# Conditioning products of a diffusion step: two stationary columns in one column group, or 32 padded columns in four

## The chip, the core and the metric

The kernel runs on one core of one Trainium2 chip. The metric is the device time of one execution in microseconds (us). The kernel before takes 1270.43 us, the median of 3 runs (1269.55 to 1271.19).

Engine names are those of the profile: PE is the matrix engine, PEld its weight loads, DVE the vector engine, ACT the scalar engine, POOL the GpSimd engine, SP the engine from whose queue nearly all DMAs here are issued. SPq is time in SP's queue. "Stationary" is the operand that a weight load puts into the array, "moving" the one that streams through it. A PSUM bank holds 512 fp32 numbers in each of 128 partitions.

## The reference

One step of a two-layer backbone: layer 0 has two attention mixers A and B, layer 1 a Fourier mixer. There are 256 context tokens and 1024 latent tokens of width 1024. Each layer starts from a normalised input that is scaled and shifted by vectors made from a conditioning vector, and ends with a gate made from it. There are two conditioning vectors, `c` for latent tokens and `c_ctx` for context tokens.

```python
def ada_mod(cvec, w, b):                       # w: (1024, 3072), one per layer
    m = jax.nn.silu(cvec) @ w + b
    return jnp.split(m, 3, axis=-1)            # shift, scale, gate

def modulate(h, shift, scale):
    return h * (1 + scale) + shift

for l in range(DEPTH):                         # DEPTH = 2
    shc, scc, gtc = ada_mod(c_ctx, ada_w[l], ada_b[l])
    shl, scl, gtl = ada_mod(c, ada_w[l], ada_b[l])
    hc = modulate(rms_norm(xc, norm_g[l]), shc, scc)
    hl = modulate(rms_norm(xl, norm_g[l]), shl[:, None], scl[:, None])
    # layer 0: projections of hc, hl; attention A (global) and B (window); gated output projection
    # layer 1: Fourier mixing of the projected input; gated output projection
    xc = xc + gtc * yc
    xl = xl + gtl[:, None] * yl
y_prompt, y_sample = rms_norm(xc, final_g), rms_norm(xl, final_g)
```

The change touches `silu(cvec) @ w` alone: a product of 2 vectors of 1024 with a 1024 x 3072 matrix, for each layer.

## The kernel before, in words

Tokens are cut into 10 tiles of 128 and three groups: tiles 0 to 3, 4 to 7 (latent) and 8 to 9 (context). Big products take their operands as a high and a low part (`mm3`, L246, three products for one); the conditioning products take plain fp32 operands.

All conditioning weights are cut into blocks of 128 columns. A block is one DMA from `ada_w` of 128 x 8 x 128 numbers, 512 KB (`ada_tile`, L461, pieces of 512 bytes), and one group of eight matmuls (`ada_mm`, L466), one for each 128 rows of the matrix: `cs[:, b, :]`, 128 x 2, is stationary, the block's 128 columns are moving, and the result stands in two partitions of a PSUM bank.

**Layer 0's shift and scale** are wanted first. A loop over `k` = 0 to 7 loads the two blocks of 128 columns (`ada_load`), multiplies them (`ada_chunk`, tile name `ada`, one bank `g`), copies the 2 x 256 result to SBUF on ACT (L480), turns it with two small transposes on PE (L483, `modt`) and writes column `k` of `modb` and `moda` on DVE (L485, L486). Then `mod_chunk` makes the modulated, split columns `k` of token group 0, and products of those columns with the first key weights and query weights are added into four banks, `kv0s`, `kv2s`, `q0s`, `q2s` (`gemm_chunk`, L492; three of these banks have the tag `s`, one the tag `a`), a few `k` behind.

**The rest of what is multiplied early** (gate of layer 0; shift and scale of layer 1; `AT_P`) is 24 blocks. `ada_fill` puts them among the following work by the table `AT_N`: that work (`S1`) normalises and modulates groups 1 and 2 (transposes `xt`, L397), loads cached keys, and makes the remaining keys, values and first queries. Each block has a bank `t` (tile name `ad`), an ACT copy (L822) and a small transpose (L799, `mt`) for a shift or a scale, or a DVE addition (L818) and a DMA to the DRAM tensor `gtd` for a gate. Layer 1's gate is made elsewhere, on DVE (class `Rows`).

**Buffers.** Weight blocks take buffers from the zones `p`, `pt` and `q` (4, 3 and 2 of them); tiles 8 and 9 of the input and some of the query work take theirs from the same zones. A load waits in SP's queue until the buffer's last reader is done, and all loads behind it wait too. Banks: `s` has 3, `t` has 3, `a` and `g` one each.

**Order.** Instructions are recorded in the order of the code, and a scheduler sets the order of each engine's queue from its own estimate of times. What stands in the queues is fixed when the program is built; on the chip each queue runs in order.

Then the attention follows (lines 860 to 1010), with remaining projections filled between its pieces, then the output projection and layer 1. None of its code is touched.

## Time and profile before

| | us |
|---|---|
| median of 3 runs | 1270.43 |
| the profiled execution's own time | 1269.79 |
| its span, first to last instruction | 1268.0 |
| PE busy, of the span | 1218.0 |
| DVE busy | 874.0 |
| ACT busy | 586.4 |
| POOL busy | 314.0 |

The 1.8 us between the profiled execution's own time and its span lie outside the instructions. The page divides the span into 40 slices of 31.7 us. PE is busy seven tenths of the first slice and at least eight tenths of almost every other; the DMA engines are at 0.9 or more in the first two slices and at 0.6 or less in most others. The chain of waits goes back from the last instruction to what released it, so its shares say what set the end.

A fp32 matmul of the program stands in the trace as two matmul records, each with its weight load, while a product of split operands stands as one. So a group of eight conditioning matmuls is 16 records. PE's records overlap (a matmul of 272 ns starts 109 ns after the one before), so what one costs is read from start to start and not from its length.

### The profile page before, as it was taken

To read this page: it belongs to the slowest core of one execution; us is meant where nothing else is said; L and a number is where in the kernel's file an instruction comes from. 1 tells how busy PE (TensorE), PEld (TensorE's weight loads), DVE (VectorE), ACT (ScalarE), POOL (GpSimd) and SP (SyncE) were. 2 spreads that over 40 slices of the span, in tenths; PEclk is the share of its full clock that TensorE was granted. 3 is DMA by queue.
4 is the path that set the end of the run, shared out by engine and by line. 5 is a ranking of instruction groups with operands and counts; after the bars stand their busy time and mean duration, and the time that the engine had idled before them with its cause. 6 is when DMAs were issued, how large, how long until landed. Compare 5 with 4: busy or idle time off the path is not lost.

```text
span 1268.0 us, 22014 instructions
## 1 busy us (share of the span) xinstructions
PE 1218.0 (96%) x8063; PEld 1073.5 (85%) x8063; DVE 874.0 (69%) x2036; ACT 586.4 (46%) x1179; POOL 314.0 (25%) x269
## 2 busy tenths in 40 slices
PE   7989999999999999999999988979999998999997
PEld 6767889999999999998999986868777888988886
DVE  3455388887767677666888868675775988558553
ACT  3332235655556455555665667432264324333121
POOL 2234155341322122010100012310412206335001
PEclk9999999999999999999999999989999999999999
DMA  9956522132342325234424379597312544355321
GB/s 298 310 146 170 164 75 63 50 114 82 107 134 75 106 65 167 57 105 117 117 67 150 89 200 250 157 255 214 124 45 75 168 148 142 101 163 172 132 84 67
DMA packets 175311, 168.83 MB, mean 133 GB/s; under 512 B 19753, under 2 KB 140373, under 8 KB 175202
## 3 DMA queue, kind: packets, MB, share of 16 engines
q1 hardware_dynamic: 175202, 167.41, 44.9%
q8 instruction: 64, 1.05, 0.3%
q14 instruction: 45, 0.37, 0.1%
HBM read 123.19 MB, written 44.18 MB: 132 GB/s over the span
## 4 chain that ended last, share of the span: by engine, by line
PE 83%; DMA 7%; DVE 4%; ACT 2%; issue 1%; POOL 1%; SPq 1%; POOLq 0%; DVEq 0%; ACTq 0%
PE ga L246 9%; PE of L246 9%; PE av L987 8%; PE pt L981 7%; PE q L246 7%; PE oz L246 6%; PE sL L864 4%; PE u L246 4%; PE kv L246 4%; PE ad L466 4%; PE g1E L246 4%; PE g1O L246 3%; PE sC L864 3%; PE ada L466 2%; PE g1c L246 2%; PE wa L516 2%
## 5 line engine op out<-in xcount | busy, mean ns | idle before, releaser
L984 DVE TENSOR_TENSOR pt<-pt,pt 128x512 fp32r<-128x512 f32 (+1 forms) x264 | 171.1, 658 | 42.8 <-ACT pt L258 42.4
L258 ACT ACTIVATE pt<-pt 128x512 fp32r<-128x512 f32 (+1 forms) x264 | 146.3, 576 | 81.5 <-PE pt L981 52.0
L987 PE MATMUL av<-pt,u 128*128 128x256 f32 x1008 | 168.7, 290 | 2.3 <-DVE e L999 1.5
L981 PE MATMUL pt<-identr,p 128*128 128x128 f32 x1008 | 154.8, 272 | 2.4 <-ACT e L962 1.3
L987 PEld LDWEIGHTS av<-pt,u 128*128 128x128 f32 x1008 | 139.6, 189 | 7.8 <-DVE e L999 3.0
L246 PE MATMUL q<-w,u 128*128 128x256 f32 x864 | 130.1, 287 | 0.3 <-ACT u L420 0.2
L981 PEld LDWEIGHTS pt<-identr,p 128*128 128x128 f32 x1008 | 118.4, 140 | 8.3 <-ACT e L962 1.5
L905 ACT ACTIVATE p<-p,nm 128x1280 f32<-128x1280 f32 (+1 forms) x80 | 95.4, 1192 | 62.6 <-DVE p L898 61.3
L246 PE MATMUL ga<-u,w 128*128 128x512 f32 (+1 forms) x576 | 124.2, 359 | 0.0
L246 PEld LDWEIGHTS q<-w,u 128*128 128x128 f32 x864 | 114.1, 189 | 4.4 <-DVE u L422 0.5
L246 PEld LDWEIGHTS ga<-u,w 128*128 128x128 f32 x576 | 93.6, 188 | 13.5
L264 POOL TENSOR_TENSOR w<-h,w 128x512 fp32r<-128x512 f32 x42 | 55.5, 1338 | 133.3 <-DVE w L260 96.7
L864 PE MATMUL sL<-u,q 128*128 128x512 f32 x256 | 81.0, 410 | 3.9 <-DMA q<-qd 2.3
L905 ACT ACTIVATE p<-p,NM 128x640 f32<-128x640 f32 (+2 forms) x80 | 59.1, 740 | 25.2 <-DVE p L898 25.0
L264 POOL TENSOR_TENSOR u<-h,u 128x512 fp32r<-128x512 f32 x19 | 25.8, 1363 | 171.4 <-ACT u L258 160.3
L246 PE MATMUL oz<-u,u 128*128 128x512 f32 x240 | 63.0, 397 | 3.4 <-DVE h L1180 1.6
L864 PE MATMUL sC<-u,q 128*128 128x256 f32 x320 | 63.2, 298 | 0.2 <-DMA q<-qd 0.2
L639 POOL TENSOR_TENSOR h<-h,rope 128x512 f32<-128x512 f32 (+1 forms) x18 | 21.7, 1206 | 148.7 <-ACT h L722 99.5
L246 PE MATMUL kv<-w,u 128*128 128x256 f32 x384 | 57.9, 289 | 0.0
L246 PEld LDWEIGHTS oz<-u,u 128*128 128x128 f32 x240 | 44.5, 188 | 14.6 <-issue 2.0
L898 DVE TENSOR_SCALAR_CACHE_REDUCE p<-sL 128x512 f32<-128x512 f32 x64 | 43.8, 684 | 18.4 <-PE sL L864 9.3
L898 DVE TENSOR_SCALAR_CACHE_REDUCE p<-sL,nm 128x512 f32<-128x512 f32 x64 | 47.6, 744 | 7.8 <-PE sL L864 6.5
(774 smaller groups left out, 2723.6 us busy)
## 6 DMA issues: line engine op xcount, KB each, us to landing
q<-qd SPq DMA_DIRECT2D x80, 256.0 KB
p<-i_ada_w SPq DMA_DIRECT2D x21, 512.0 KB
h<-i_w_in SPq DMA_DIRECT2D x40, 256.0 KB
h<-i_w_out SPq DMA_DIRECT2D x32, 256.0 KB
pt<-i_ada_w SPq DMA_DIRECT2D x14, 512.0 KB
qd<-q SPq DMA_DIRECT2D x22, 256.0 KB
w<-i_wuT SPq DMA_DIRECT2D x8, 512.0 KB
u<-i_x SPq DMA_DIRECT2D x8, 512.0 KB
```

The lines of the kernel that those rows point to most:

```text
L246: pe.matmul(out, a, b, start=i == 0, stop=i == n - 1)
L258: act.activation(out, in_, AF.Copy)
L264: pick("lo" + lc, lc).tensor_sub(dst_l, src, dst_h)
L466: pe.matmul(out, cs[:, b, :], raw[:, b, :], start=b == 0, stop=b == 7)
L516: pe.matmul(acc[:, i * 256 : i * 256 + 256], wu[j][:, c0 : c0 + P], f[:, j, :], start=j == 0, stop=j == 1)
L639: pick("rope", XE["rope"]).tensor_mul(t1.rearrange("p t h (b c) -> p t (h b) c", b=2), y.rearrange("p t h (b c) -> p t (h b) c", b=2), cb)
L864: pe.matmul(ps, q_at(q, s, hc), keys, start=s == 0, stop=s == 1)
L898: dve.tensor_scalar(p[i][:, end[i] : end[i] + n], ps, sign, last[i], op0=ALU.mult, op1=ALU.min, accum_out=c)
L905: act.activation(p[i][:, 0 : end[i]], p[i][:, 0 : end[i]], AF.Exp, bias=last[i], scale=-1.0, accum_out=SU[:, t, hd + i, 0:1],)
L981: pe.transpose(tp[:, jj * 256 + i * P : jj * 256 + i * P + P], p[i][:, off : off + P], ident)
L984: dve.tensor_sub(pt[:, 1, 0:n], tp[:, 0:n], pt[:, 0, 0:n])
L987: pe.matmul(acc, vv, pt[:, s, jj * 256 : jj * 256 + 256], start=c + jj + s == 0, stop=c + jj == nt - 1 and s == 1,)
```

## The change

The two vectors are padded to 32 columns with zeros (`csw`, one memset on POOL and one copy on DVE at the start). The result of a matmul then fills 32 partitions, and four matmuls that use the same 128 rows of the matrix but four different blocks of 128 columns write the four quarters of one bank's partitions: in the array they stand in four column groups of 32. In the built program the matmuls before have the same kind of placement, 128 rows by 32 columns, always at column 0; now it is at columns 0, 32, 64 and 96.

For layer 0's shift and scale the loop takes two `k` at once: four loads of 128 x 4 x 256 (pieces of 1 KB), 32 matmuls in the order row block, then column group, one ACT copy of 128 x 128, one 128 x 128 transpose and three DVE operations for both `k`. For the rest there are 24 loads of 128 x 2 x 512 (pieces of 2 KB) and 8 matmuls for each; four such steps fill one bank, now of tag `s`, which is then copied, turned and written like above, or, for the gate, added to the bias in four quarters. Number of matmuls (320) and of weight loads by DMA (40 of 512 KB) stay.

```diff
+AT_B = "s"
...
     dve.tensor_scalar(cs, cs, 0.5, None, op0=ALU.mult)
+    csw = take("e", (P, 8, 32))
+    pool.memset(csw.a, 0.0)
+    dve.tensor_copy(csw[:, :, 0:2], cs)
...
-    def ada_tile(l, part, k, tags):
-        raw = take(tags, (P, 8, P))
-        c0 = part * D + k * P
-        sp.dma_start(raw.a, I["ada_w"][l, :, c0 : c0 + P].rearrange("(b p) c -> p b c", p=P))
-        return raw
-
-    def ada_mm(out, raw):
+    def ada_mm(ps, j, b, raw, start, stop):
+        pe.matmul(ps[32 * j : 32 * j + 32, 0:P], csw[:, b, :], raw, start=start, stop=stop)
+
+    def ada_mods(l, name, ps, fill):
+        row = take("e", (P, P))
+        act.activation(row.a, ps[:, 0:P], AF.Copy)
+        tp = t_bank(name)
+        pe.transpose(tp[:, 0:P], row.a, ident)
+        drop(row)
+        fill(tp[:, 0:P].rearrange("p (j v) -> p j v", j=4)[:, :, 0:2])
+
+    def mod_shift(l, k, n, tv):
+        bb = bT[:, l, k : k + n].unsqueeze(2).to_broadcast([P, n, 2])
+        dve.tensor_add(modb[:, l, k : k + n, :], tv, bb)
+
+    def mod_scale(l, k, n, tv):
+        bb = bT1[:, l, k : k + n].unsqueeze(2).to_broadcast([P, n, 2])
+        gb = gT[:, l, k : k + n].unsqueeze(2).to_broadcast([P, n, 2])
+        dve.tensor_add(moda[:, l, k : k + n, :], tv, bb)
+        dve.tensor_mul(moda[:, l, k : k + n, :], moda[:, l, k : k + n, :], gb)
+
+    def ada_load(kk):
+        out = []
+        for hb in range(2):
+            for part in range(2):
+                raw = take(("p", "pt", "q"), (P, 4, 256))
+                c0 = part * D + kk * 256
+                sp.dma_start(
+                    raw.a, I["ada_w"][0, hb * 512 : hb * 512 + 512, c0 : c0 + 256].rearrange("(b p) c -> p b c", p=P)
+                )
+                out.append(raw)
+        return out
+
+    def ada_chunk(kk, raws):
+        ps = bank("g", f"ada{kk}")
         for b in range(8):
-            pe.matmul(out, cs[:, b, :], raw[:, b, :], start=b == 0, stop=b == 7)
-        drop(raw)
...
+            for j in range(4):
+                part, i = divmod(j, 2)
+                raw = raws[b // 4 * 2 + part]
+                ada_mm(ps, j, b, raw[:, b % 4, i * P : i * P + P], b == 0, b == 7)
+        drop(*raws)
+
+        def fill(tv):
+            mod_shift(0, 2 * kk, 2, tv[:, 0:2])
+            mod_scale(0, 2 * kk, 2, tv[:, 2:4])
+
+        ada_mods(0, f"modt{kk}", ps, fill)
...
-    todo_ada = deque((l, part, k) for l, part in AT_P for k in range(8))
...
+    todo_ada = deque((l, part, h, s) for l, part in AT_P for h in range(2) for s in range(4))
+    open_ada = []
+
+    def ada_step(l, part, h, s):
+        raw = take(AT_Z, (P, 2, 512))
+        c0 = part * D + h * 512
+        sp.dma_start(raw.a, I["ada_w"][l, s * 256 : s * 256 + 256, c0 : c0 + 512].rearrange("(b p) c -> p b c", p=P))
+        if s == 0:
+            open_ada.append(bank(AT_B, f"ad{l}{part}{h}"))
+        ps = open_ada[0]
+        for i in range(2):
+            for j in range(4):
+                ada_mm(ps, j, 2 * s + i, raw[:, i, j * P : j * P + P], s + i == 0, s + i == 4)
+        drop(raw)
+        if s < 3:
+            return
+        open_ada.pop()
+        if part < 2:
+            ada_mods(l, f"mt{l}{part}{h}", ps, lambda tv: (mod_shift, mod_scale)[part](l, 4 * h, 4, tv))
+            return
+        row, bias = take("e", (P, P)), take("e", (P, P))
+        for j in range(4):
+            c1 = 2 * D + h * 512 + j * P
+            sp.dma_start(bias[32 * j : 32 * j + 2, :], I["ada_b"][l, c1 : c1 + P].partition_broadcast(2))
+        for j in range(4):
+            rows = slice(32 * j, 32 * j + 2)
+            dve.tensor_add(row[rows, :], ps[rows, 0:P], bias[rows, :])
+            sp.dma_start(gtd[l, :, h * 512 + j * P : h * 512 + j * P + P], row[rows, :])
+        drop(row, bias)
```

The lines left out are the old loop bodies and the calls (`if k % 2 == 0:` ahead of the loads and of `ada_chunk`).

The scheduler orders the queues anew as far as the middle of the attention on A; from there PE's order is the same but for a few rows. Three places are shown. A row is the line, the operation, the written and the read tile with their buffer numbers, the size of the output, and how many equal instructions follow each other.

**PE, in the loop of layer 0's shift and scale.** `ada` are the conditioning products, `modt` the turn of their result, `kv0s`, `kv2s`, `q0s`, `q2s` the products of token group 0. Before, two groups of eight and the work around them:

```order
L492 MATMUL q0s<-w_333,u_434 128x256
L483 MATMUL modt_494<-identr,e_492 128x2 x2
L466 MATMUL ada_554<-p_550,cs 2x128 x8
L466 MATMUL ada_554<-pt_552,cs 2x128 x8
L492 MATMUL q0s<-w_334,u_434 128x256
L492 MATMUL q0s<-w_333,u_435 128x256
```

Now, the end of one set of 32 and the start of the next:

```order
L464 MATMUL ada_401<-q_399,e_115 32x128 x2
L464 MATMUL ada_401<-pt_397,e_115 32x128 x2
L464 MATMUL ada_401<-q_399,e_115 32x128 x2
L470 MATMUL modt_436<-identr,e_434 128x128
L464 MATMUL ada_537<-p_529,e_115 32x128 x2
L516 MATMUL kv0s<-w_301,u_441 128x256
L516 MATMUL kv0s<-w_302,u_441 128x256
```

Each row of two is two column groups that read the same load. 33 separate runs of conditioning products stood on PE's queue, and 25 stand there now.

**PE, around the last products of token group 0.** `xt` are the transposes of token group 1, each tile of four waited for by ACT and DVE, which make the modulated columns from it. Before, the transposes stand behind the last of the `kv0s` to `q2s` products and a gate block (`ad`):

```order
L492 MATMUL q2s<-w_333,u_578 128x256
L492 MATMUL q2s<-w_334,u_578 128x256
L492 MATMUL q2s<-w_333,u_579 128x256
L466 MATMUL ad_833<-q_829,cs 2x128 x7
L397 MATMUL xt_846<-identr,u_467 128x128
L397 MATMUL xt_846<-identr,u_468 128x128
L397 MATMUL xt_846<-identr,u_469 128x128
L397 MATMUL xt_846<-identr,u_470 128x128
L397 MATMUL xt_855<-identr,u_467 128x128
```

Now five of the eight sets of `xt` stand ahead of the last 48 of these products, and the other three among them or right behind:

```order
L401 MATMUL xt_843<-identr,u_470 128x128
L401 MATMUL xt_843<-identr,u_471 128x128
L401 MATMUL xt_843<-identr,u_472 128x128
L401 MATMUL xt_843<-identr,u_473 128x128
L516 MATMUL kv0s<-w_301,u_577 128x256
L516 MATMUL kv0s<-w_302,u_577 128x256
L516 MATMUL kv2s<-w_301,u_577 128x256
L516 MATMUL kv2s<-w_302,u_577 128x256
```

No gate block stands before the end of these products any more; three did.

**PE and ACT, at the first block of the gate.** Before, on PE (`ckt` is the turn of cached keys, `xt_981` belongs to token group 2):

```order
L397 MATMUL xt_915<-identr,u_470 128x128
L617 MATMUL ckt_927<-identr,h_924 128x128 x2
L466 MATMUL ad_938<-p_934,cs 2x128 x8
L466 MATMUL ad_953<-pt_949,cs 2x128 x8
L466 MATMUL ad_968<-q_964,cs 2x128 x8
L397 MATMUL xt_981<-identr,pt_761 128x128
```

Now (`q_1325` are the queries of token group 2):

```order
L250 MATMUL q_1325<-w_323,u_936 128x256
L464 MATMUL ad_772<-p_770,e_115 32x128 x8
L464 MATMUL ad_772<-pt_781,e_115 32x128 x8
L464 MATMUL ad_772<-q_791,e_115 32x128 x8
L464 MATMUL ad_772<-p_891,e_115 32x128 x8
L401 MATMUL xt_989<-identr,pt_732 128x128
```

The new tile `ad_772` has the bank in which `q0s` stood, so its first matmul waits for the second ACT row that reads `q0s`. ACT before, where the first tile read out is `kv0s`, ahead of token group 1:

```order
L258 ACTIVATE u_775<-ckt_779 64x256
L666 ACTIVATE pt_1069<-kv0s 128x512
L649 ACTIVATE q_1071<-pt_1069 128x256
L420 ACTIVATE u_844<-xt_846,modb,moda 128x512
L417 ACTIVATE h_860<-xt_855,modb,moda 128x512
```

ACT now, where `q0s` is the first, among the pieces of token group 2:

```order
L424 ACTIVATE u_936<-xt_938,modb,moda 128x256
L421 ACTIVATE h_948<-xt_945,modb,moda 128x256
L748 ACTIVATE h_1073<-q0s 128x512
L424 ACTIVATE u_936<-xt_952,modb,moda 128x256
L421 ACTIVATE h_962<-xt_959,modb,moda 128x256
L424 ACTIVATE u_966<-xt_968,modb,moda 128x256
L675 ACTIVATE h_1076<-q0s 128x512
```

All of token group 1 now stands ahead of the first read of these four banks.

More of the change, by code (lines that the diff above doesn't have):

```diff
@@ L456, in htile @@
         return hcols(gi, k, (t - GROUPS[gi][0]) * P, P)
-    def ada_tile(l, part, k, tags):
-        raw = take(tags, (P, 8, P))
-        c0 = part * D + k * P
-        sp.dma_start(raw.a, I["ada_w"][l, :, c0 : c0 + P].rearrange("(b p) c -> p b c", p=P))
-        return raw
-    def ada_mm(out, raw):
-        for b in range(8):
-            pe.matmul(out, cs[:, b, :], raw[:, b, :], start=b == 0, stop=b == 7)
-        drop(raw)
-    def ada_load(k):
-        out = []
-        for part in range(2):
-            out.append(ada_tile(0, part, k, ("p", "pt", "q")))
-        return out
@@ L475, in ada_chunk @@
-    def ada_chunk(k, raws):
-        ps = bank("g", f"ada{k}")
-        for part, raw in enumerate(raws):
-            ada_mm(ps[0:2, part * P : part * P + P], raw)
-        row = take("e", (2, 256))
-        act.activation(row.a, ps[0:2, 0:256], AF.Copy)
-        tp = t_bank(f"modt{k}")
-        for part in range(2):
-            pe.transpose(tp[:, 2 * part : 2 * part + 2], row[:, part * P : part * P + P], ident[0:2, 0:2])
-        drop(row)
-        dve.tensor_scalar(modb[:, 0, k, :], tp[:, 0:2], bT[:, 0, k : k + 1], None, op0=ALU.add)
-        dve.tensor_scalar(moda[:, 0, k, :], tp[:, 2:4], bT1[:, 0, k : k + 1], gT[:, 0, k : k + 1], op0=ALU.add, op1=ALU.mult)
+    def ada_mm(ps, j, b, raw, start, stop):
+        pe.matmul(ps[32 * j : 32 * j + 32, 0:P], csw[:, b, :], raw, start=start, stop=stop)
@@ L556, in hybrid_step @@
     for k in range(8):
-        ada = ada_load(k)
+        if k % 2 == 0:
+            ada = ada_load(k // 2)
         if k == AT_K:
@@ L569, in hybrid_step @@
             raws = raw_T(0)
-        ada_chunk(k, ada)
+        if k % 2 == 0:
+            ada_chunk(k // 2, ada)
         hh, hl = h_slot(0, k)
@@ L791, in q0 @@
         fl_.run(lambda: q_pair(0, 0, t, wqa0, "ga"[n % 2]), ("q", t, 0))
-    todo_ada = deque((l, part, k) for l, part in AT_P for k in range(8))
-    turn_later = deque()
-    def ada_turn():
-        l, part, k, row = turn_later.popleft()
-        tp = t_bank(f"mt{l}{part}{k}")
-        pe.transpose(tp[:, 0:2], row[:, 0, :], ident[0:2, 0:2])
-        drop(row)
-        b = bT[:, l, 8 * part + k : 8 * part + k + 1]
-        if part == 0:
-            dve.tensor_scalar(modb[:, l, k, :], tp[:, 0:2], b, None, op0=ALU.add)
-        else:
-            dve.tensor_scalar(moda[:, l, k, :], tp[:, 0:2], bT1[:, l, k : k + 1], gT[:, l, k : k + 1], op0=ALU.add, op1=ALU.mult)
+    todo_ada = deque((l, part, h, s) for l, part in AT_P for h in range(2) for s in range(4))
@@ L807, in ada_fill @@
     def ada_fill(n):
         for _ in range(min(n, len(todo_ada))):
-            l, part, k = todo_ada.popleft()
-            raw = ada_tile(l, part, k, AT_Z)
-            row = take("e", (2, 2, P))
-            sl = slice(k * P, k * P + P)
-            if part == 2:
-                sp.dma_start(row[:, 1, :], I["ada_b"][l, part * D + k * P : part * D + k * P + P].partition_broadcast(2))
-            ps = t_bank(f"ad{l}{part}{k}")
-            ada_mm(ps[0:2, 0:P], raw)
-            if part == 2:
-                dve.tensor_add(row[:, 0, :], ps[0:2, 0:P], row[:, 1, :])
-                sp.dma_start(gtd[l, :, sl], row[:, 0, :])
-                drop(row)
-            else:
-                act.activation(row[:, 0, :], ps[0:2, 0:P], AF.Copy)
-                turn_later.append((l, part, k, row))
@@ L824, in ada_fill @@
-            while len(turn_later) > 1:
-                ada_turn()
+            ada_step(*todo_ada.popleft())
     for n, op in enumerate(S1):
@@ L845, in hybrid_step @@
     ada_fill(len(todo_ada))
-    while turn_later:
-        ada_turn()
+    drop(csw)
     ws["qa1"] = load_w(w0cols(C_QA + 256))
```

## The prediction, made before the changed kernel was run

> **What bounds the kernel now.** First the page: busy times, and the chain of waits by engine and by line.
>
> ```profile
> PE 1218.0 (96%) x8063; PEld 1073.5 (85%) x8063; DVE 874.0 (69%) x2036; ACT 586.4 (46%) x1179; POOL 314.0 (25%) x269
> PE 83%; DMA 7%; DVE 4%; ACT 2%; issue 1%; POOL 1%; SPq 1%; POOLq 0%; DVEq 0%; ACTq 0%
> PE ga L246 9%; PE of L246 9%; PE av L987 8%; PE pt L981 7%; PE q L246 7%; PE oz L246 6%; PE sL L864 4%; PE u L246 4%; PE kv L246 4%; PE ad L466 4%; PE g1E L246 4%; PE g1O L246 3%; PE sC L864 3%; PE ada L466 2%; PE g1c L246 2%; PE wa L516 2%
> ```
>
> PE sets the end, and the conditioning products (`ad` 4%, `ada` 2%) are 6% of the chain, some 75 us. All lie ahead of the attention, so I cut that stretch where its work changes (columns: stretch, its length, busy time and number of records for each engine, granted clock, DMA share, GB/s).
>
> ```profile
> core 0: us, PE busy (x) PEld busy (x) DVE busy (x) ACT busy (x) POOL busy (x), PEclk, DMA share, GB/s
> 5.00:10.00 5.00, 4.19 (x10) 3.42 (x11) 0.00 (x0) 1.23 (x3) 0.00 (x0) 1.00 1.02 378
> 10.00:57.00 47.00, 45.16 (x345) 35.40 (x345) 23.47 (x46) 17.97 (x33) 12.58 (x10) 0.96 1.07 306
> 57.00:71.00 14.00, 14.00 (x121) 11.80 (x120) 5.55 (x12) 4.28 (x8) 1.96 (x2) 1.00 1.12 310
> 65.00:75.00 10.00, 10.00 (x86) 8.76 (x85) 3.15 (x8) 1.89 (x4) 0.70 (x1) 1.00 1.17 292
> 71.00:82.40 11.40, 11.40 (x93) 9.65 (x93) 2.52 (x10) 2.16 (x4) 1.92 (x3) 1.00 0.68 181
> 82.40:94.10 11.70, 6.54 (x49) 4.78 (x48) 9.33 (x15) 6.10 (x9) 7.92 (x8) 0.90 0.01 4
> 94.10:108.80 14.70, 14.41 (x98) 10.10 (x98) 8.44 (x24) 6.79 (x15) 5.81 (x5) 0.85 0.47 133
> 108.80:167.50 58.70, 58.70 (x484) 47.33 (x483) 27.04 (x76) 9.96 (x30) 17.51 (x19) 1.00 0.58 164
> ```
>
> To 71 us (the layer 0 loop) PE and the DMA engines are both full. To 82.4 us PE finishes token group 0. From 82.4 to 94.1 it idles 5.2 us while DVE, busy 9.3 of 11.7, works at token group 1. From there to the first scores of the attention, at 167.5 us, it never rests. What it saves here moves all that follows forward; what follows is PE's too.
>
> **What a group costs.** The chain in order of time (start, length, who) and one view of the `ada` tile:
>
> ```profile
> 14.97 3.58 PE ada L466 x32
> 18.56 1.13 PE xt L397 x9
> 19.69 1.84 PE ada L466 x16
> 26.30 6.87 DMA p<-i_ada_w
> 44.58 0.21 PE modt L483 x2
> 48.93 0.70 PE q2s L492 x6
> 94.22 7.52 PE ad L466 x48
> 110.13 5.33 PE ad L466 x48
> 116.48 0.15 PE mt L799
> L466 PEld LDWEIGHTS ada<-p,cs x112: 80/85/129, 14.9 to 70.7; 128*2 128x2 f32 x112
> L466 PE MATMUL ada<-p,cs x112: 270/272/421, 14.9 to 70.8; 128*2 128x128 f32 x112
> ```
>
> Three groups take 5.33 us and one 1.84: (5.33 - 1.84) / 32 records is 109 ns for a record, 218 ns for a matmul of two, and entering a run costs 1.84 - 16 x 0.109 = 0.10 us. The 40 groups are 40 x 1.74 = 69.8 us, and 33 runs 3.3 us more.
>
> **What four column groups make of it.** No row shows two column groups at work at once; the price of a matmul is bounded. The nearest rows are layer 1's narrow products, in the timeline of PE:
>
> ```profile
> 1125.40 0.24 PE L1602 MATMUL pn<-alt,nyq 128*4 128x2 f32 x4
> 1125.51 0.64 PE L1606 MATMUL p<-u,alt 128*2 128x128 f32 x8
> 1125.98 0.64 PE L1606 MATMUL p<-w,alt 128*2 128x128 f32 x8
> ```
>
> Four records with two moving columns start within 1125.40 to 1125.51, 26 ns or so each: as fast as records can be issued. Eight with 128 moving columns take 0.47 us, 59 ns each; the fp32 records' 109 ns are nearly twice that, so a record is bound by what streams and not by its issue. If four groups overlap freely, a matmul costs its two issues, 52 ns; if none do, 218. The two records of one matmul use the same column group and stand next to each other, the next matmul's two use another. If records start in order, the second waits until the first has streamed (109 ns), and only then may the next group's first start beside it. A matmul then costs 109 ns and at most one issue, 109 to 135 ns. I take 122, the middle, because in every row PE's records start in order.
>
> The weights grow from 2 to 32 columns. A load of 2 lasts 85 ns; one of 128:
>
> ```profile
> L246 PEld LDWEIGHTS q<-w,u 128*128 128x128 f32 x864 | 114.1, 189 | 4.4 <-DVE u L422 0.5
> ```
>
> That is 0.8 ns a column, 110 ns for 32, an estimate. PEld's loads overlap the matmuls as they do at 189 ns, so I price the padding at nothing; without that cover it is 640 x 25 ns = 16 us. The memset and copy that make the padded columns are done before 14.9 us, while PE is in the `wa` products.
>
> [...]
>
> **The sum**, against the profiled execution's own 1269.8 us (0.6 under the median shown):
>
> 1. Products: 320 x (218 - 122) ns = **-30.7 us**. In the layer 0 loop that is 128 matmuls, 12.3 us: the loop would end at 71 - 12.3 = 58.7 us. Does the DMA allow it? Ahead of and with its last block stand 17.7 MB in SP's queue (x tiles 0 to 7, 16 blocks, `wuT`, key and query weights, `rope`, `wcd` and `wsd`): at 306 GB/s 58 us. Pieces of 1 KB instead of 512 bytes should make it less: with pieces of 4 KB (5 to 10 us) the rate is 378, with 512 bytes mostly (65 to 75 us) 292. I take 57. So PE and DMA end together, and nothing is lost.
> 2. Runs: 33 - 25 = 8 fewer at 0.10 us = **-0.8**.
> 3. Turns of the result: 8 pairs `modt` at 0.21 and 16 `mt` at 0.15 are 4.1 us. 8 transposes remain, at 0.12 or 0.13 (the `xt` row above: 1.13 / 9), and some 0.06 of change on each side, 1.5: **-2.6**. ACT's copies and DVE's small additions fall in number; neither engine bounds, so they count nothing.
> 4. The pause at 82.4 to 94.1 us, 5.2 us, and behind it a clock of 0.85, at which 48 records take 7.52 instead of 5.33 us: 7.4 us in all. The waits there:
>
> ```profile
> PE ckt L617 <- DVE h L421: 3.5, 1, 3.5
> PE xt L397 <- ACT h L417: 1.2, 2, 0.7
> PE xt L397 <- DVE h L421: 0.5, 1, 0.5
> ```
>
>    The transposes of token group 1 now stand ahead of the last 48 products of group 0, which cover them (48 x 0.117, by the `q2s` row above, 5.6 us). But these products queue behind the transposes, and need `mod_chunk` 6 and 7 from ACT and DVE, which have group 1 in between. I keep 3.4 us of pause: **-4**.
> 5. The new wait for a bank. The gate's first matmul needs ACT's second read of `q0s`, which stands behind five pieces of token group 2 and another read; on PE, behind it, wait the rest of `q` and all of `kv` for group 1:
>
> ```profile
> L420 ACT ACTIVATE u<-xt,modb,moda 128x256 fp32r<-128x256 f32 x4 | 2.3, 569 | 7.0 <-PE xt L397 7.0
> L649 ACT ACTIVATE h<-q0s 128x512 f32<-128x512 f32 x1 | 0.6, 595 | 0.0
> ```
>
>    Seven rows, 4.0 us on ACT; meanwhile PE has 12 products and 14 transposes, 12 x 0.117 + 14 x 0.125 = 3.2 us. With ACT's delay, **+2**.
> 6. Loads. Nine buffers, two held by x tiles 8 and 9: seven steps can be loaded ahead, and PE asks for nine in its first 72 matmuls of the gate. Two loads come late by a 512 KB transfer each, 1.4 to 1.8 us at 378 to 292 GB/s: **+3**. In SP's queue the x loads, cached keys and `qa1` weights keep their place among the loads; the eight bias loads and eight `gtd` writes go in fours.
>
> Sum: -30.7 - 0.8 - 2.6 - 4 + 2 + 3 = -33.1, so 1236.7, and 0.6 on the median: **1237 us**. The first scores would start near 134 instead of 167.5 us. Behind them PE has the same products in a somewhat different order, which I price at nothing since PE is full there.
>
> **Rivals.**
>
> *A: the groups overlap freely*, 52 ns a matmul: 320 x 166 = 53.1 us. The loop would end at 71 - 21.2 = 49.8 us, but its last block lands at 57, so 7 us are lost. 1269.8 - 53.1 + 7 - 0.8 - 2.6 - 4 + 2 + 3 = 1221, **1222** on the median. For it: issue at 26 ns leaves room. Against it: the pair on one group. [...]
>
> *C: no overlap at all.* The moving columns of all four groups may come through one stream, as they do in every row here. The products keep 218 ns, and the rest of the sum, -2.4, remains: **1268**, hardly a change.
>
> *D: each change of column group empties the array.* A run's entry costs 0.10 us in the chain rows, and the products change group at each matmul. 320 x 0.10 = 32 us on top of C's sum: **1300**, slower. It decides from 8 ns a change if nothing overlaps, from 104 if the overlap saves 96. For it: something at the edge of a run costs that much. Against it: the edge also changes from 128 columns to 32, and inside a run nothing changes size. [...]
>
> **How the numbers follow.** My forecast 0.47, A 0.25, C 0.18, D 0.10. The forecast's own range is 1230 to 1247: 109 to 135 ns are 4 us either way, and terms 4 to 6 some 5. For 8 in 10 the range takes in A and what lies between forecast and C: 1217 to 1265. A difference under 0.2% (2.5 us) cannot be told from none. C is as often just faster as the same. Faster: 0.47 + 0.25 + 0.09 = 0.81; same 0.09; slower 0.10.
>
> **What would show it.** Start to start in a run of conditioning products: 61 ns a record for the forecast, 26 for A, 109 for C, over 130 for D. The loop's last product at 57 to 60 us; a wait for the bank before `ad` of 1 to 3 us; waits of `ad` on `i_ada_w` of some 3 us; the first scores near 134 us; from there the same length as before, within 4 us. I am wrong if the products get cheaper and the first scores do not move by about as much, or if they move and the rest grows.

## The result, and the profile after

| | before | changed |
|---|---|---|
| median, us | 1270.41 | 1232.40 |
| ratio, 95% interval | 1 | 0.9712 (0.967 to 0.9754) |
| single times, us | 1269.55 to 1271.19 | 1230.34, 1232.29, 1232.51, 1240.12 |
| profiled execution, its span, us | 1268.0 | 1238.3 |
| granted clock over that span | 0.990 | 0.976 |

The change makes the kernel 38 us faster; the forecast was 1237 us. The profiled execution of the changed kernel is the longest of its four, so its span is only 29.7 us shorter. First the page of the changed kernel: busy times, and the chain of waits by engine.

```profile
PE 1177.0 (95%) x8039; PEld 1048.1 (85%) x8039; DVE 868.8 (70%) x2023; ACT 580.4 (47%) x1163; POOL 313.9 (25%) x270
PE 71%; DMA 13%; DVE 8%; ACT 3%; issue 2%; SPq 1%; POOL 1%; POOLq 0%; DVEq 0%; ACTq 0%
```

PE works 41 us less. Its share of the chain falls from 83% to 71%, and those of the DMA and of DVE nearly double. Where they come in is seen in the same stretches as before the change (columns as in the prediction; the last one ends where the second tile of scores starts).

```profile
10.00:57.00 47.00, 38.67 (x433) 31.11 (x431) 22.16 (x46) 17.78 (x33) 14.09 (x11) 0.96 1.05 346
57.00:71.00 14.00, 11.61 (x81) 10.96 (x82) 9.66 (x17) 8.24 (x13) 6.11 (x6) 0.88 0.80 277
71.00:82.40 11.40, 9.62 (x120) 7.88 (x119) 9.46 (x19) 9.05 (x18) 6.84 (x6) 1.00 0.01 2
82.40:94.10 11.70, 9.49 (x172) 8.59 (x173) 7.21 (x28) 1.20 (x4) 7.61 (x9) 1.00 0.90 307
94.10:108.80 14.70, 14.21 (x213) 11.71 (x212) 14.20 (x37) 4.11 (x10) 5.58 (x6) 1.00 0.99 352
108.80:131.10 22.30, 20.15 (x198) 18.80 (x196) 17.33 (x38) 4.57 (x11) 11.75 (x12) 1.00 0.60 178
```

Before, PE was all but full in every stretch except 82.4 to 94.1 us; now it has gaps of 1.8 us or more in all but one (94.1 to 108.8, where it idles 0.5). In the layer 0 loop (to 57 us) it does 433 records instead of 345 and still idles 8.3 of 47 us, while the DMA engines are full. From 71 to 82.4 us the DMA engines stand still, and from 82.4 to 108.8 they are full again.

The two executions are compared where the same number of matmuls is left. That is the start of the second tile of scores, 175.0 us before and 131.1 now. The same view over two stretches, of the kernel before:

```profile
10.00:175.00 165.00, 156.83 (x1233) 125.38 (x1232) 83.64 (x194) 49.08 (x102) 52.54 (x48) 0.97 0.71 200
175.00:1268.00 1093.00, 1056.98 (x6821) 944.69 (x6821) 789.82 (x1836) 534.32 (x1073) 260.44 (x215) 0.99 0.41 122
```

and of the changed kernel:

```profile
10.00:131.10 121.10, 103.75 (x1209) 89.05 (x1207) 80.02 (x182) 44.95 (x87) 51.98 (x48) 0.97 0.82 272
131.10:1238.00 1106.90, 1068.79 (x6820) 955.58 (x6819) 788.11 (x1834) 533.02 (x1073) 260.62 (x214) 0.98 0.40 120
```

To that point PE is busy 53.1 us less and idle 17.4 us instead of 8.2, so it arrives 43.9 us earlier. Behind it the same work takes 13.9 us longer in this execution: the granted clock is lower there. The length of each 10 us window times (1 - its granted clock) adds up to 26 us instead of 8, and the window from 800 us is at 0.54. The other three executions have clocks of 0.979 to 0.982 and spans 8 to 10 us shorter.

How a group of products runs now is seen in the timeline of PE, in the loop (start, length of the piece, records):

```profile
16.54 0.30 PE L464 MATMUL ada<-pt,e 128*32 128x128 f32 x2 [1.00 <-DMA pt<-i_ada_w]
16.55 0.30 PE L464 MATMUL ada<-p,e 128*32 128x128 f32 x2
16.67 0.28 PE L464 MATMUL ada<-pt,e 128*32 128x128 f32 x2
16.68 0.28 PE L464 MATMUL ada<-p,e 128*32 128x128 f32 x2
```

Four records start together, one for each column group, and the next four some 0.12 us later: 30 ns a record where it was 109. The chain of the changed kernel in order of time shows this and what takes the place of PE:

```profile
80.49 1.88 PE ad L464 x64
...
83.11 6.31 DMA pt<-i_ada_w
...
89.51 3.93 DMA e<-i_ada_b
...
96.52 6.10 DMA p<-i_ada_w
...
104.52 0.57 PE ad L464 x16
...
130.20 0.44 DVE h L681
...
131.18 0.68 PE sL L889 x2
```

Sixty-four records take 1.88 us and 16 take 0.57, so a record costs (1.88 - 0.57) / 48 = 27.3 ns and a matmul 55 ns, and entering a run still costs 0.13 us. But between the products the chain now runs over loads of weight blocks and of a bias row, and the scores wait for DVE.

PE's waits from 10 to 132 us in the changed kernel (what waited for what: us in total, times, longest):

```profile
PE kv0s L516 <- ACT u L424: 3.3, 3, 1.5
PE ad L464 <- DMA p<-i_ada_w: 2.4, 2, 2.2
PE xt L401 <- DVE u L650: 1.9, 1, 1.9
PE kT L643 <- DVE h L681: 1.9, 1, 1.9
```

With the shorter ones the view lists 5.7 us of waits for weight blocks and some 11 us for DVE and ACT.

### The profile page after: what moved, and what is told of

Read it like the earlier page. It is cut to its first block, busy times and chain, and to the rows that moved or that the text cites. A ratio compares the mean times of both kernels' runs of the same rounds, so it can differ in the third digit from the quotient of the medians.

```text
span 1238.3 us, 21899 instructions
## 1 busy us (share of the span) xinstructions
PE 1177.0 (95%) x8039; PEld 1048.1 (85%) x8039; DVE 868.8 (70%) x2023; ACT 580.4 (47%) x1163; POOL 313.9 (25%) x270
## 4 chain that ended last, share of the span: by engine, by line
PE 71%; DMA 13%; DVE 8%; ACT 3%; issue 2%; SPq 1%; POOL 1%; POOLq 0%; DVEq 0%; ACTq 0%
PE of L250 9%; PE ga L250 8%; PE av L1012 7%; PE pt L1006 7%; PE q L250 6%; PE oz L250 6%; PE sL L889 4%; PE g1E L250 4%; PE u L250 3%; PE g1O L250 3%; PE kv L250 2%; PE sC L889 2%; DMA h<-i_w_out 2%; DMA q<-qd 2%; DMA u<-i_x 1%
## 5 line engine op out<-in xcount | busy, mean ns | idle before, releaser
L1012 PEld LDWEIGHTS av<-pt,u 128*128 128x128 f32 x1008 | 141.5, 191 | 7.9 <-DVE e L1024 2.1
L250 PE MATMUL q<-w,u 128*128 128x256 f32 x864 | 133.0, 289 | 1.5 <-DVE u L426 1.2
L268 POOL TENSOR_TENSOR w<-h,w 128x512 fp32r<-128x512 f32 x42 | 56.7, 1369 | 124.6 <-DVE w L264 88.1
L250 PEld LDWEIGHTS oz<-u,u 128*128 128x128 f32 x240 | 44.5, 188 | 12.9 <-ACT h L262 1.3
L889 PEld LDWEIGHTS sC<-u,q 128*128 128x128 f32 x320 | 50.0, 193 | 4.1 <-issue 0.8
```

Of the source, the lines that this page charges most:

```text
L250: pe.matmul(out, a, b, start=i == 0, stop=i == n - 1)
L268: pick("lo" + lc, lc).tensor_sub(dst_l, src, dst_h)
L889: pe.matmul(ps, q_at(q, s, hc), keys, start=s == 0, stop=s == 1)
L1012: pe.matmul(acc, vv, pt[:, s, jj * 256 : jj * 256 + 256], start=c + jj + s == 0, stop=c + jj == nt - 1 and s == 1,)
```

## The experiments

My theory from this comparison was that the four column groups overlap fully, which PE's 52 us show, and that 14 of the 52 (52 less the 38 by which the median fell) are lost to waits for loads and for DVE and to the granted clock. Each run is compared with runs of the kernel before on the same chip. Times alone tell little under 0.5%, because the granted clock changes from run to run (0.980 to 0.991 in 13 runs of the kernel before). Span times mean granted clock hardly changes: for the kernel before it is 1250 to 1257 us in 13 runs whose times spread from 1265.7 to 1282.5. I call it the length at full clock and give its mean over a kernel's runs.

| run | median us | ratio (95%) | at full clock | second tile of scores, us |
|---|---|---|---|---|
| kernel before, three series | 1269.9, 1271.6, 1268.8 | 1 | 1254.0, 1252.7, 1253.5 | 175.0 |
| changed kernel | 1232.4 | 0.9712 (0.967 to 0.9754) | 1206.8 | 131.1 |
| e5_after_again | 1234.2 | 0.9687 (0.9656 to 0.9717) | 1209.8 | 132.0 |
| e1_one_group | 1264.4 | 0.9947 (0.991 to 0.9984) | 1246.0 | 164.4 |
| e2_two_groups | 1241.8 | 0.9771 (0.9696 to 0.9847) | 1220.0 | 141.5 |
| e3_same_group_next | 1235.0 | 0.9717 (0.966 to 0.9774) | 1212.5 | 136.4 |
| e12_sixteen_together | 1244.9 (one run) | | 1217.0 | 142.2 |
| e4_half_loop_loads | 1220.9 | 0.9616 (0.9565 to 0.9666) | 1198.5 | 123.5 |
| e6_half_fill_loads | 1226.4 | 0.9655 (0.9605 to 0.9706) | 1205.9 | 127.0 |
| e8_late_fold | 1232.0 | 0.9674 (0.9637 to 0.9712) | 1210.5 | 124.8 |
| e9_half_all_loads | 1221.2 | 0.9609 (0.9574 to 0.9644) | 1198.5 | 124.4 |
| e11_one_group_half_loads | 1263.9 | 0.9956 (0.9933 to 0.9979) | 1243.8 | 164.0 |
| e7_early_fills | 1230.8 | 0.9664 (0.9632 to 0.9697) | 1208.9 | 128.0 |
| e10_early_fills_one_add | 1228.1 | 0.9678 (0.9649 to 0.9706) | 1209.0 | 128.8 |

### One column group, and two

The products of the changed kernel with the four of a step on one column group:

```diff
-        pe.matmul(ps[32 * j : 32 * j + 32, 0:P], csw[:, b, :], raw, start=start, stop=stop)
+        c0 = j // 1 * P
+        pe.matmul(ps[32 * (j % 1) : 32 * (j % 1) + 32, c0 : c0 + P], csw[:, b, :], raw, start=start and j < 1, stop=stop and j >= 3)
...
-        act.activation(row.a, ps[:, 0:P], AF.Copy)
+        for m in range(4):
+            act.activation(row[32 * m : 32 * m + 32, :], ps[0:32, m * P : m * P + P], AF.Copy)
```

> All four products of a step go to column group 0, one behind the other, each into 128 columns of its own of the bank; loads, padding and order stay. Four copies in place of one carry the result on, and the gate's additions get a copy ahead: eight times some 0.75 us more on ScalarE, off the path. Theory (the gain is the overlap of four column groups, 55 ns a matmul with it): a record costs 109 ns again, a group of 16 records 1.8 us where it took 0.57, a matmul 218 ns; 320 x 163 = 52 us more on TensorE, of which the 8 to 14 us are free that TensorE now waits for loads and for VectorE: 1270 to 1277 us. Rival (a good part of the gain comes from the wider loads and the fewer runs and turns, and not from the overlap): below 1262 us.

One row of its chain:

```profile
99.87 13.65 PE ad L465 x124
```

A record costs 110 ns again, as the theory says. The time, 1264.4 us, is neither the theory's 1270 to 1277 nor the rival's under 1262. At full clock the kernel is 8.0 us shorter than the kernel before: that is what the wider blocks, fewer runs and turns and the other order bring without any overlap, less whatever the added copies cost (PE waits 1.4 us for their result in the loop). The overlap itself is worth 1246.0 - 1206.8 (or 1209.8), that is 36 to 39 us.

Two column groups, each with two ranges of the bank:

```diff
-        pe.matmul(ps[32 * j : 32 * j + 32, 0:P], csw[:, b, :], raw, start=start, stop=stop)
+        c0 = j // 2 * P
+        pe.matmul(ps[32 * (j % 2) : 32 * (j % 2) + 32, c0 : c0 + P], csw[:, b, :], raw, start=start and j < 2, stop=stop and j >= 2)
```

> Column groups 0 and 1 alone, each taking two of the four products into two ranges of the bank; the rest as in the changed kernel. Theory (each column group is a stream of its own, so the price of a record is 109 ns divided by the groups in use): four records in 109 ns become two, 55 ns a record, 110 ns a matmul, a group of 16 records 0.95 us or so; 320 x 55 = 17.6 us more on TensorE, of which the 128 matmuls of the layer 0 loop (7 us) lie under its loads: 1240 to 1248 us. Rival (something other than the number of groups sets the 27 ns a record, their issue for instance): the price stays under 35 ns a record and the time within 3 us of 1232.

```profile
99.20 1.00 PE ad L465 x16
...
104.72 1.87 PE ad L465 x32
```

In these rows of its chain the second 16 records of a run cost 0.87 us, 54 ns each. So one, two and four groups gave 110, 54 and 27.3 ns: 110 / 54 = 2.0 and 110 / 27.3 = 4.0, the number of groups in use. The time, 1241.8 us, lies in the theory's range and outside the rival's.

### Which records may pass which

```diff
-        for b in range(8):
+        for hb in range(2):
             for j in range(4):
...
+                for b in range(4 * hb, 4 * hb + 4):
...
-        for i in range(2):
-            for j in range(4):
+        for j in range(4):
+            for i in range(2):
```

> The same matmuls on the same four column groups, but those of one group stand together: 4 matmuls (8 records) of a group in the layer 0 loop, 2 matmuls (4 records) in the later products, where the changed kernel goes to the next group after every matmul (2 records). [...] Rival N (a record can pass only a few that stand right ahead of it): 4 records of a group then cost 3 x 109 + 27 ns at least, 88 ns a record in the later products (192 matmuls, 2 x 61 ns more each, 23 us) and 99 in the loop (128 matmuls, 2 x 72 ns, 18 us of which 7 lie under loads): 1258 to 1268 us.

From its chain, first two rows of the loop (8 records of a group together), then one of the later products (4 together):

```profile
43.89 2.39 PE ada L464 x32
...
52.60 1.47 PE ada L464 x16
...
110.67 0.59 PE ad L464 x16
```

The time, 1235.0 us, is far under rival N's 1258, and with 4 records of a group together, 16 take 0.59 to 0.67 us, hardly more than the 0.57 to 0.64 of the changed kernel. But with 8 together, 16 over two groups take 1.47 and 32 over four take 2.39: 75 to 92 ns a record. PE's timeline shows where the starts lie. In a set of 32 the first two groups read one block (`p`) and the other two the next (`pt`). The set at 43.82 us has its first `pt` record, the third group's, at 44.75, and three `p` records, the second group's last, start behind it, at 44.86, 44.97 and 45.08. So two groups hold the third back by 0.93 us, some 0.46 each. If every group's first record starts right behind the fifth of the eight before it, 4 x 0.109 = 0.44 us after their first, an estimate is 0.44 + 8 x 0.109 + 0.1 = 1.4 us for two groups and 3 x 0.44 + 0.87 + 0.1 = 2.3 for four. The loop's last product comes 7 us later, and the kernel is 3 to 6 us longer at full clock: 256 records at some 90 instead of 27 ns are an estimated 16 us, and the rest of them, as I read it, lies under waits for loads; no run separates it.

The one run of 64 in this order, with 4 together, takes 2.48 us (at 85.75 us in the chain) where the changed kernel's takes 1.88; what the 0.6 us are, no run shows.

Whether the order makes a record dearer with 8 together, or the wait for blocks, can be tested by making the pieces longer:

```diff
-        for b in range(8):
-            for j in range(4):
+        for j in range(4):
+            for b in range(8):
```

> In the layer 0 loop all 8 matmuls of a column group stand together (16 records), then those of the next group; the later products are as in the changed kernel. With 8 records of a group together, 16 records over two groups took 1.46 us and 32 over four 2.39; with 4 together 16 took 0.59 to 0.67, as with 2. [...] Rival (what slowed the groups of 8 was the wait for blocks, not the order): 64 records take 2 to 4 us. One record after the other would be 7.0 us.

No group of 64 ran without a wait in it, since its second blocks come late. Two runs of 56 did. If a group's first record starts here too with three of the one before still to start, 4 x 0.109 = 0.44 us after the first of 8 and 12 x 0.109 = 1.31 after the first of 16, an estimate is 0.44 + 2 x 1.31 + 16 x 0.109 + 0.1 = 4.9 us. The chain has

```profile
52.38 5.03 PE ada L464 x56
```

for one and 5.01 us for the other; with 27 ns a record it would be 1.6, and one after the other 6.1. These 56 waited for no block and take more than the 2 to 4 us that the rival has for 64, so the order costs this. The timeline of PE shows its first starts:

```profile
52.31 0.73 PE L464 MATMUL ada<-pt,e 128*32 128x128 f32 x5
52.77 0.30 PE L464 MATMUL ada<-p,e 128*32 128x128 f32 x1
52.88 0.27 PE L464 MATMUL ada<-pt,e 128*32 128x128 f32 x1
52.91 0.27 PE L464 MATMUL ada<-p,e 128*32 128x128 f32 x1
52.99 0.27 PE L464 MATMUL ada<-pt,e 128*32 128x128 f32 x1
53.02 0.27 PE L464 MATMUL ada<-p,e 128*32 128x128 f32 x1
53.09 0.27 PE L464 MATMUL ada<-pt,e 128*32 128x128 f32 x1
```

Eight records of one group (`pt`) are at the head of the queue. The next group's first (`p`, 52.77) starts behind the fifth of them, ahead of the last three, although it stands behind all eight in program order. The first records of the next two groups start at 54.11 and 55.45 us, 1.34 us apart.

### What the loads take back

Half of the loop's blocks:

```diff
-        for hb in range(2):
+        for hb in range(1):
...
-                raw = raws[b // 4 * 2 + part]
+                raw = raws[part]
```

> In the layer 0 loop only the first half of each pair of weight blocks is loaded (8 blocks of 512 KB in place of 16) and used twice: half of the conditioning sum of layer 0 is left out, the products are as many as before. Theory (since the products are cheap, the DMA sets the end of the layer 0 loop, and half of what the last step saved was lost there): 4.2 MB less at the 346 GB/s of this stretch is 12 us; the waits of ada on its blocks (6.7 us in all) go, the loop's last product comes at 48 to 52 us in place of 56.7, the x tiles of group 2 land some 10 us earlier, and the time falls by 5 to 10 us: 1222 to 1227 us. Rival (the loop's end is set by the chain over VectorE and ScalarE, and the loads only look late): the last product within 2 us of 56.7 and the time within 2 us of 1232.

Its last weight load for a loop product (the changed kernel's came at 56.6 us, in the same view by tile):

```profile
L464 PEld LDWEIGHTS ada<-pt,e x96: 106/110/154, 16.3 to 46.6; 128*32 128x32 f32 x96
```

It ends 10 us earlier, the second tile of scores starts 7.6 us earlier, and the kernel is 8 to 11 us shorter at full clock. The theory holds, with an end of the loop and a time (1220.9 us) a little under the ranges it gave. The DMA sets the end of the loop, and of the 21 us that its 128 products save (128 x 163 ns) 8 to 11 are lost.

Half of the later products' blocks:

```diff
-        raw = take(AT_Z, (P, 2, 512))
+        raw = take(AT_Z, (P, 1, 512))
...
-        sp.dma_start(raw.a, I["ada_w"][l, s * 256 : s * 256 + 256, c0 : c0 + 512].rearrange("(b p) c -> p b c", p=P))
+        sp.dma_start(raw.a, I["ada_w"][l, s * 256 : s * 256 + 128, c0 : c0 + 512].rearrange("(b p) c -> p b c", p=P))
...
-                ada_mm(ps, j, 2 * s + i, raw[:, i, j * P : j * P + P], s + i == 0, s + i == 4)
+                ada_mm(ps, j, 2 * s + i, raw[:, 0, j * P : j * P + P], s + i == 0, s + i == 4)
```

> The 24 weight blocks of the later products (gate of layer 0, shift and scale of layer 1) are loaded half, 256 KB each, and used twice: half of those sums is left out, the products are as many as before. 6.3 MB less, 18 us at 346 GB/s. In the changed kernel the DMA engines are full from 80 to 114 us, and TensorE waits 2.9 us there for blocks. Theory F (these loads set the pace up to the first scores): the waits go, the second tile of scores starts at 126 to 129 us in place of 131.1, and the time falls by 2 to 5 us. Rival V (VectorE sets the start of the scores, busy 14.6 of the 17.0 us ahead of them and 9.6 of 9.7 from 94.8 to 104.5): the waits go, but the second tile of scores starts within 1.5 us of 131.1 and the time stays within 2 us.

At full clock it is 4 us shorter than the changed kernel in the same series, and the second tile of scores starts 4 to 5 us earlier. That is the theory's size; the medians differ by more, 7.8 us, with a clock of 0.983 against 0.9822 and the spread of the runs in it. The waits of these products for blocks shrink to 1.4 us but do not go. The runs of the two kernels overlap (1203.7 to 1209.9 us at full clock against 1206.9 to 1213.2), so the 4 us are the least certain of these differences.

Fewer bytes in the loop without leaving anything out: the first fold product is made later, with the other three.

```diff
-EF = 1
+EF = 0
```

> The first of the four fold products (32 records wa ahead of the layer 0 loop, with 1.3 MB of loads and 1.0 MB of writes) moves behind the attention's start to the other three. Theory (the layer 0 loop ends when its bytes have come, 346 GB/s): 2.3 MB less are 6.7 us; the loop's last conditioning product comes 4 to 7 us earlier than 56.7, the second tile of scores 3 to 6 us earlier than 131.1; 32 records of 0.12 us are 4 us more for TensorE behind it, where it is full, so the time changes by -2 to +1 us. Rival (the x tiles and the work on VectorE set the loop's end): its last product within 2 us of 56.7, and the time 3 to 5 us longer.

```profile
L464 PEld LDWEIGHTS ada<-p,e x112: 106/110/178, 11.6 to 50.0; 128*32 128x32 f32 x112
```

The loop's products end at 50.0 us, 6.6 earlier, and the second tile of scores starts 6 to 7 us earlier (3 to 6 were expected). But the 32 records come back behind it, and the length at full clock is 1210.5 against 1209.8: the theory's answer, and no gain.

Now all loads halved, with four groups and with one (both edits above, the second on the kernel with one group):

> Both edits that halve loads at once: 8 blocks of 512 KB in place of 16 in the layer 0 loop, 24 of 256 KB in place of 512 KB for the later products, each used twice; half of every conditioning sum is left out, the products are as many as in the changed kernel. 10.5 MB less, 30 us at 346 GB/s. Theory (of the 52 us that TensorE saves, what does not arrive is lost to loads: 8 us in the loop, 4 to 5 at the later products, which add up because they lie in different stretches): span times clock falls to 1193 to 1199 us from 1207 to 1210, the second tile of scores starts at 117 to 121 us in place of 131 to 132. Rival V (behind the loads stands VectorE's work on keys and queries, which has to be done before the scores and is not shortened): the two savings do not add up, 1199 to 1203 us, the second tile at 122 to 125.

> The same halved loads, but all four products of a step on column group 0, one behind the other: against the run with halved loads and four groups it gives what the overlap is worth where loads do not bind. With full loads it was worth 36 to 38 us at full clock (1245.5 for one group, 1207 to 1210 for four). Theory: TensorE's 218 ns a matmul hide the loads already, so halving them gains little here, 0 to 3 us: 1242 to 1246 us at full clock; the difference to four groups with halved loads is then 45 to 52 us, near the 52 that the records' price gives. Rival V: the difference stays at 36 to 42 us, because the work on VectorE takes what the loads gave.

To the second tile of scores, four groups with halved loads:

```profile
10.00:124.40 114.40, 101.47 (x1202) 89.09 (x1200) 81.50 (x179) 44.49 (x88) 53.93 (x47) 0.94 0.61 199
```

and one group with halved loads:

```profile
10.00:164.00 154.00, 148.22 (x1201) 137.59 (x1199) 79.61 (x187) 51.13 (x112) 53.07 (x47) 0.98 0.45 147
```

At full clock the overlap is worth 1243.8 - 1198.5 = 45 us here, against 36 to 39 with full loads. So loads cost 6 to 9 of the 52 us, or up to 3 more, since PE still waits for the halved loads. For one group the halving brings 2 us, so there they were hidden. The savings of the two edits do not add up: 1198.5 is what the loop's loads alone gave. It lies at the edge of both ranges expected of e9, but the second tile of scores, at 124.4 us, is where rival V put it. PE still idles 12.9 us with four groups, 5.8 with one. The waits in the same stretches, four groups first, then one:

```profile
PE ad L464 <- DMA pt<-i_ada_w: 2.0, 2, 1.5
PE xt L401 <- ACT h L421: 1.9, 3, 0.7
PE sL L889 <- DVE u L650: 1.7, 1, 1.7
```

```profile
PE xt L401 <- ACT h L421: 1.6, 4, 0.4
PE sL L892 <- DVE u L652: 1.5, 1, 1.5
```

All rows of these views together: 9.1 us for DVE and ACT and 3.6 for blocks with four groups, 5.2 and 0.7 with one. The difference, 6.8 us (3.9 for DVE and ACT, 2.9 for blocks), is about what is missing from 45 to 52. This is read from one execution of each and not tested by a run of its own.

### The granted clock

The changed kernel once more, unchanged, beside the kernel before.

> The changed kernel itself once more, in more runs, beside the kernel before on the same chip. In the profiled executions the second tile of scores starts 44 us earlier (131.1 in place of 175.0 us), but the span is only 30 us shorter; the stretches at half clock behind it cost 26 us in place of 8. Span times mean granted clock is 1205 to 1209 us in each of the four runs of the changed kernel and 1250 to 1257 in those of the kernel before, so 47 us are saved at full clock. Theory K (the change itself makes half-clock stretches more frequent): the changed kernel's mean clock lies 0.005 or more under that of the kernel before in the same series, and the ratio stays near 0.971. Rival S (these stretches come and go from run to run in either kernel): the mean clocks agree within 0.003, and the ratio falls to 0.963 to 0.967, 1224 to 1229 us on a chip where the kernel before takes 1270.

The mean clock is 0.9822 in its 6 runs and 0.9854 in 11 runs of the kernel before: a difference of 0.0032, under the 0.005 of theory K and a little over the 0.003 of rival S. The ratio, 0.9687, lies between theirs. For the other kernels with two or four column groups, and for the first series of the changed kernel, the mean lies between 0.979 and 0.9854. In the three series of the kernel before it is 0.9871, 0.9854 and 0.9884, and for one column group 0.9858 and 0.9849. A difference of 0.003 is 4 us of 1235. The change may cost some clock, but one kernel's runs spread over 0.010, and these runs leave it open. At full clock the change saves 43 us in this series.

### Towards a faster version

In the changed kernel the DMA engines stand still from 71 to 82.4 us because the blocks in the buffers wait for PE to use them: one load (L825) waits 15.7 us in SP's queue for the `ad` products. The later products are handed out earlier, on a bank that is free, and the four bias loads move from the end of a group to its first block:

```diff
-AT_B = "s"
+AT_B = ["g", "g", "s", "s", "s", "s"]
-AT_N, AT_Z = (0, 0, 3, 0, 3, 2, 2, 2, 2, 2, 3, 3, 3), ("p", "pt", "q")
+AT_N, AT_Z = (4, 0, 4, 0, 2, 2, 2, 2, 2, 2, 2, 2, 0), ("p", "pt", "q")
...
-        if s == 0:
+        if s == 0 and part == 2:
+            open_bias.append(take("e", (P, P)))
+            ...
+        if s == 0:
```

> A version that may beat both: the first two groups of later products use the bank that is free since the layer 0 loop (g) in place of one that must wait for ScalarE, they are handed out ahead of the work on token group 1, where TensorE idles (61 to 66 and 73.6 to 80.4 us: 4 us idle) and the DMA engines stand still (0.00 of their share from 73.6 to 80.4 us), and the bias rows of the gate are loaded when its first block is asked for. Theory (loads stand still there because TensorE doesn't yet free their buffers, and the stretch to the first scores is then paced by those loads): the DMA engines are at work between 66 and 80 us, the second tile of scores starts 4 to 8 us earlier, and the time falls by as much: 0.963 to 0.968 of the kernel before if the changed kernel is at 0.971. Rival V (VectorE sets the start of the scores): the loads come earlier, the scores do not, and the time stays within 2 us of the changed kernel's.

In the stretch from 66 to 80 us, where the DMA share was 0.20:

```profile
66.00:80.00 14.00, 12.16 (x191) 10.07 (x189) 9.59 (x23) 5.46 (x10) 10.18 (x9) 1.00 0.85 289
```

The loads run there now and the second tile of scores starts 3 to 4 us earlier, a little less than the theory wanted. The kernel's time does not follow clearly: 1230.8 against 1234.2 us, and 1208.9 against 1209.8 at full clock. PE's longest wait behind the loop is now `sL` for DVE, 2.7 us. So DVE was asked for less:

```diff
-        for j in range(4):
-            rows = slice(32 * j, 32 * j + 2)
-            dve.tensor_add(row[rows, :], ps[rows, 0:P], bias[rows, :])
+        dve.tensor_add(row.a, ps[:, 0:P], bias.a)
```

One memset on POOL sets the bias tile to zero first.

> The version with early later products, early bias loads and the free bank, and in it VectorE's four additions of 2 x 128 for a half of the gate (0.29 us each) become one of 128 x 128 over all rows (bias rows that are not loaded are zero): six small additions fewer, 1.7 us of VectorE between 60 and 95 us. Theory (with the loads early, VectorE sets the start of the scores: the one wait of TensorE over 2 us there is sL for VectorE): the second tile of scores starts 1 to 2 us ahead of the 128.0 of the version with four additions, the ratio to the kernel before is 0.962 to 0.967. Rival (those additions lie in gaps of VectorE): 128 and the same ratio, 0.966 or so.

The second tile starts at 128.8 and the ratio is 0.9678: there is no gain, as the rival had it, so those additions lie in gaps. Both versions have the lowest medians with nothing left out, but their intervals overlap the changed kernel's. No version here is shown to beat it.

## Why the prediction was right, and what in it was wrong

The time, 1232.4 us, lies 4.6 under the forecast and inside its own range. That the number is so near is in good part luck. The products saved 52 us of PE's time and not 30.7, and everything else 8.0 at full clock and not 2.4. Against that, 13 to 16 of the 52 us did not reach the time, and another 5 to 10 lie between the gain at full clock (43 to 48 us) and the gain in the medians (37 to 38). The forecast had none of these four in its sum at that size, and they nearly cancel.

**The step that failed is the price of a matmul in term 1.** It was taken as 122 ns, "because in every row PE's records start in order", so that the second record of a pair holds back the next group's first. It costs 55: the first records of all four groups start at 16.54 and 16.55 us, the second ones some 0.12 us later, so the second record of a pair does not hold back the next group's first. The order was read in rows in which only one column group is at work. Instead of 30.7 us PE saves 320 x (218 - 55) = 52. Of the signs that the prediction named, rival A's 26 ns a record is what the trace shows (27.3). That 26 ns is as fast as records can be issued was my reading of one row; no run shows such a limit.

**The end of the loop** was right: the prediction put the landing of the last block at 57 us and A's loss there at 7. The loop's last product comes at 56.7 us, and halving the loads gives back 8 to 11. But "PE and DMA end together, and nothing is lost" failed with the price: PE would have been done sooner.

**Terms 2 and 3** (runs and turns, -3.4) and the part of term 4 that hangs on the order were measured together with one column group: 8.0 us at full clock, where all terms but the first gave 2.4. What the 5.6 us more are was not taken apart. (Term 3 with its own figures, 8 x (0.125 + 2 x 0.06), leaves 2.0 us and not 1.5; half a microsecond.)

**Term 4, the pause**, was to shrink to 3.4 us. It moved instead, and grew. From 57 to 94.1 us PE idles 6.4 us where it idled 5.2: 4.0 from 71 on, and 2.4 from 57 to 71, at a clock of 0.88, where it was full before. From 94.1 to 108.8 us, at a clock of 0.85 before, it is now 1.00. Which part comes from the cheaper products and which from the order, no run shows.

**Term 5, the bank**, +2 us: PE's waits hold none for a bank that ACT reads; this cost nothing. **Term 6, late loads**, +3: the two waits of `ad` for blocks are 2.4 us, the right size. But the chain behind them runs over loads for most of 83 to 103 us, and halving them gives 4 us.

**Padding** was priced at nothing, with 110 ns for a weight load of 32 columns. The load takes 106 to 111 ns, and since four of them overlap too (four start at 16.54 and 16.55 us), a record still costs 27 ns.

**The first scores** were to start near 134 us and start at 119.9; the second tile, at 131.1, stands behind a wait of 1.9 us for DVE. **"From there the same length as before, within 4 us"** failed in the profiled execution: from the first scores it is 1118.4 us now and was 1100.5. Less the 26 and 8 us that the lower clock costs, both are 1092, so apart from the clock it holds.

**Rival A** had the price of a record (26 ns; 27.3 measured), and its sum is nearly right where the clock is set aside: it saves 48.5 us, and 43 to 48 were measured at full clock (1252.7 to 1209.8 in the one series; 1255.3, the profiled execution, to 1206.8 in the other). That too is partly luck: A put the products at 46 us, 53.1 less 7, and the rest at 2.4, where 36 to 39 and 8.0 were measured. What separates its 1222 us from the 1232.4 is the clock, which no rival had. **Rivals C and D** are excluded: C by the price, D because the group changes at every matmul and a record still costs 27 ns. The 0.13 us at the entry of a run stay, as D's argument about the edge had it.

## What to carry to other kernels

Here products with 32 stationary columns gained a factor of 4.0 from four column groups (110 to 27.3 ns a record) with two records of one group together. With four together 16 records took 0.59 to 0.67 us instead of 0.57 to 0.64, and with eight a record cost 75 to 92 ns. Once an engine's work has become four times cheaper, ask in each stretch what it was hiding: here 13 to 16 of 52 us were taken back, 6 to 9 of them by loads, as the runs with halved loads show, and the rest, as the waits suggest, by what loads were left and by work on VectorE and ScalarE. When differences between two runs of such a kernel are under 1%, multiply span by granted clock before comparing them.

## What the runs showed of the hardware that I had not expected

- PE's records on different column groups did not all start in program order, though the opening has each queue run in order. With 16 records of one group together, the next group's first record starts at 52.77 us, ahead of three that stand before it (52.88, 52.99 and 53.09); with 8 together, at 44.75 us, ahead of the three at 44.86, 44.97 and 45.08. This is said of starts alone, since ends are modelled in the trace.
- The price of an fp32 record with 128 moving columns is 110, 54 and 27.3 ns on one, two and four column groups, so weight loads of 32 columns (106 to 111 ns each) overlap each other as well.
- The granted clock of one and the same kernel varies between 0.978 and 0.993 from run to run (38 runs of the kernel before), and its times spread over 1.3% (1265.7 to 1282.5 us); the product of span and clock stays within 0.4% of the mean of its series.
